# Two-layer attention decoder in float32: the last three heads of layer A projected as q/k of two, q/k of one, values of three; shorter steps in layer A; both transposes ahead of both value products in layer B

## The chip, the cores and the metric

The kernel runs on one core of a Trainium2 chip. The metric is the device time of one execution in microseconds. In the profile PE is TensorE (matrix products), DVE is VectorE, ACT is ScalarE, POOL is GpSimd and SP is the engine that issues all loads of weights.

## The reference

A residual stream of 256 tokens and 1024 columns passes through two layers in float32. Layer A is causal differential attention with 8 heads of 2 x 64 columns, layer B dilated attention in 8 head pairs with three groups of keys; each is followed by an MLP with squared ReLU. Cut to what matters:

```python
# layer A, 8 heads
q, k, v = jnp.split(rms_norm(x, a_norm) @ w_qkv, 3, axis=-1)
q = apply_rope(rms_norm(q, q_gain)); k = apply_rope(rms_norm(k, k_gain))
p = softmax(mask(q @ k.T) * D ** -0.5)          # two maps per head
a = p[:, :, 0] - lam * p[:, :, 1]
o = rms_norm(a @ v, sub_gain) * (1 - lam_init)
x = x + o @ w_o
x = x + square(relu(rms_norm(x, m_norm) @ w_up)) @ w_down
# layer B, three dilation groups; k and v projected from x
o_g, lse_g = softmax attention of group g
o = sum over g of softmax_g(lse)[g] * o_g
x = x + o @ w_o                                   # and the MLP again
```

## The kernel before

Every product of float32 matrices is made of three products of rounded halves: high by high, high by low, low by high (L300 to L302). So each weight tile is split after its load, the high half by ACT (L86) and the low half by VectorE (L87); the same is done with activations (`split`, L346).

Work is driven by the projection. `gemm` (L305) makes one projection in parts; after each part `tick` (L217) is called. A tick splits up to two halves of weights ahead (`W.pump`) and advances each attention generator that is due by one step. A generator `yield`s the number of ticks until its next step, so WAIT_A and WAIT_B say how much projection lies between the steps of a head. The order of TensorE is the order of the code; the orders of the other engines are made by the framework's scheduler, which also may place a `high_priority` piece earlier.

In layer A a head has 48 products of 384 columns (q and k of two maps, 256 columns, and values, 128) with four ticks, one after each 12 products. `rows_A` (`qk_rows`, L317) turns the q/k columns into normed, rotated rows: squares on ACT, a product `T` with the rope table and a reduction on VectorE (L324, L328), then on POOL an add (L335), a power `f` (L339) and a scaling `qn` (L341); there are two such row sets per head, one for each block of 128 tokens. `values_A` splits the values. `attn_A` (L525) has five steps: transposes of q and k on TensorE (L364) and their split `th`, `tl`; scores (L357), mask, exponentials and the combination `smA` (L550); transposes of the softmax weights (L555) and their split `pA`; value products (L566, L567), their sum `orow`, and its norm on POOL (`ms` L578, `ors` L580) and ACT (L582); transposes of the output (L586). Heads 0 to 5 run like this. The last two heads, 6 and 7, have q/k of both in one projection of 512 columns (`Aqk`), then the values of both in one of 256 (`Av`). For a width other than 384 `gemm_half` has one more tick between the two token blocks, so that a step is 6 products of 512 columns or 12 of 256. Then the output projection (`OutProj`, L409 to L411) runs in bodies of 12 products of 512 columns with two ticks each; heads 6 and 7 come last, in `group`.

Layer B goes through 8 head pairs, each with q, k and values of 48 products of 384 columns. `attn_B` (L598): q/k transposes, two steps of scores, then for each of the two heads of the pair transposes of the weights (L629), their split `p`, and the value products (L643), sums on ACT, VectorE and POOL (L646 to L648), and at the end the split `oTh`, `oTl`, which the output projection reads.

PSUM is a pool of eight buffers that all tiles of TensorE's results share; the last values `v` of three heads have three buffers in SBUF.

```python
        yield WAIT_A[0] + 3 * (hd == KT - 1)
...
            yield WAIT_B[4 + hh]
```

Of the kernel before, what the change touches and what calls it, by code (L numbers as in the profile page):

```python
# [16 lines left out]
P = 128  # L17
# [3 lines left out]
KT = DM // P  # L21
HD = 64
# [14 lines left out]

WAIT_A = (3, 2, 4, 3, 4)  # L40
WAIT_B = (4, 2, 2, 5, 3, 3)

SUB = ((2, 0, 4), (3, 1, 5))

# [62 lines left out]
def trunk(ctx, tc, a):  # L107
# [17 lines left out]
    def plan(key, src, n):  # L125
        at[key] = len(chunks)
        chunks.append((src, n))
# [5 lines left out]
            if j > 0:  # L133
                plan(("dn", layer, j - 1), a["wdn"][layer, j - 1], 2 * DM)

    for hd in range(KT - 2):
        for i in range(2):
            plan(("A", hd, i), a["wA"][hd, i], 4 * 384)
    for i in range(2):
        plan(("Aqk", i), a["wAqk"][i], 4 * 512)  # L140
    plan(("Av", 0), a["wAv"], 8 * 256)
    for i in range(4):
        plan(("oA", i), a["woA"][i], 2 * DM)
    plan_mlp(0)
# [72 lines left out]
    def tick():  # L217
        W.pump()
        for ent in list(active):
            if ent[1] > 0:  # L220
                ent[1] -= 1
                continue
            try:
                ent[1] = next(ent[0]) - 1
            except StopIteration:
                active.remove(ent)

    def start(gen):
        ent = [gen, 0]
        active.append(ent)  # L230
        return ent
# [57 lines left out]
    def gemm_half(pss, h, key, j, i, n, nk=2):  # L289

        wh, wl = W.get(at[(*key, j)], i)
        for t in range(NT):
            if t and n != 384:
                tick()
            tok = slice(t * P, (t + 1) * P)
            ps = pss[t][:, :n]
            for k in range(nk):
                kt = nk * (2 * j + i) + k
                c = slice(k * n, (k + 1) * n)
                nc.tensor.matmul(ps, h[:, kt, 0, tok], wh[:, c], start=kt == 0, stop=False)  # L300
                nc.tensor.matmul(ps, h[:, kt, 0, tok], wl[:, c], start=False, stop=False)  # L301
                nc.tensor.matmul(ps, h[:, kt, 1, tok], wh[:, c], start=False, stop=kt == KT - 1)  # L302
        W.release(at[(*key, j)], i)
# [219 lines left out]


    def attn_A(hd, qr, kr, vt, oh, ol):  # L525
        yield WAIT_A[0] + 3 * (hd == KT - 1)
        T = qk_T(qr, kr, (0, P))
        yield WAIT_A[1]
        nm = small.tile([P, 4], F32, name="nm", tag="nm")
        den = small.tile([P, 2, 2], F32, name="den", tag="den")  # L530
        sm = wk.tile([P, 2, 3 * P], F32, name="smA", tag="sm")
        scs = [wps(), wps()]
        scores2([sc[:, 0:S] for sc in scs], T, block(1), KALL)
        scores2([sc[:, S:S + P] for sc in scs], T, block(0), slice(S, S + P))
        for c in range(2):
            sc = scs[c]
            masked(sm[:, c, 0:S], sc[:, 0:S], mask[:, 8:10, :].rearrange("p b k -> p (b k)"),
                   nm[:, 2 + c:3 + c])
            masked(sm[:, c, S:S + P], sc[:, S:S + P], mask[:, 9, :], nm[:, c:c + 1])
        for c in range(2):  # L540
            for q, cols in ((1, slice(0, S)), (0, slice(S, S + P))):
                nc.scalar.activation(sm[:, c, cols], sm[:, c, cols], AF.Exp, bias=nm[:, 2 * q + c:2 * q + c + 1],
                                     scale=-1.0, accum_out=den[:, q, c:c + 1])

        cf = small.tile([P, 2, 2], F32, name="cf", tag="cf")
        nc.vector.reciprocal(cf[:, :, 0], den[:, :, 1])
        nc.vector.scalar_tensor_tensor(cf[:, :, 0], cf[:, :, 0], nlam, den[:, :, 0], op0=ALU.mult, op1=ALU.mult)
        nc.scalar.activation(cf[:, :, 1], den[:, :, 0], AF.Square, scale=EPS ** 0.5)
        for q, cols in ((1, slice(0, S)), (0, slice(S, S + P))):
            nc.vector.scalar_tensor_tensor(sm[:, 0, cols], sm[:, 1, cols], cf[:, q, 0:1], sm[:, 0, cols],  # L550
                                           op0=ALU.mult, op1=ALU.add)
        yield WAIT_A[2]
        pp = wps()
        for i in range(3):
            nc.tensor.transpose(pp[:, block(i)], sm[:, 0, block(i)], ident)  # L555
        p2 = wk.tile([P, 2, 3, P], F32R, name="pA", tag="p2")
        ph, pl = p2[:, 0], p2[:, 1]
        with tc.high_priority(100):
            split(ph, pl, pp[:, :384].rearrange("p (b q) -> p b q", b=3))
        yield WAIT_A[3]  # L560
        po = wps()
        for q in range(2):
            o2 = po[:, q * 2 * P:(q + 1) * 2 * P]
            for j in range(q + 1):
                b = j if q else 2
                nc.tensor.matmul(o2, ph[:, b], vt[:, j], start=j == 0, stop=False)  # L566
                nc.tensor.matmul(o2, pl[:, b], vt[:, j], start=False, stop=j == q)  # L567
        pov = po.rearrange("p (q l d) -> p q l d", q=2, l=2)
        oc = wk.tile([P, 2, P], F32, name="oc", tag="sq")
        nc.scalar.activation(oc, pov[:, :, 1, :], AF.Copy)  # L570
        orow = wk.tile([P, 2, P], F32, name="orow", tag="oT")
        nc.vector.tensor_tensor(orow, pov[:, :, 0, :], oc, op=ALU.add)
        oss = small.tile([P, 2], F32, name="oss", tag="oss")
        for q in range(2):
            nc.scalar.activation(oc[:, q, :], orow[:, q, :], AF.Square, scale=P ** -0.5,
                                 accum_out=oss[:, q:q + 1])
        ms = small.tile([P, 8], F32, name="ms", tag="ms")
        nc.gpsimd.tensor_tensor(ms[:, :2], oss, cf[:, :, 1], op=ALU.add)  # L578
        ors = small.tile([P, 2], F32, name="ors", tag="ors")
        nc.gpsimd.tensor_tensor(ors, ms[:, :2], half[:, :2], op=ALU.pow)  # L580
        for q in range(2):
            nc.scalar.activation(orow[:, q, :], orow[:, q, :], AF.Copy, scale=ors[:, q:q + 1])  # L582
        yield WAIT_A[4]
        pt = wps()
        for q in range(2):
            nc.tensor.transpose(pt[:, block(q)], orow[:, q, :], ident)  # L586

        ptv = pt[:, :S].rearrange("p (m h l) -> p h m l", h=2, l=2)
        for t in range(NT):
            o = oh[:, hd, block(t)].rearrange("p (m l) -> p m l", l=2)  # L590
            nc.scalar.activation(o, ptv[:, t], AF.Copy, scale=sgain)
            nc.vector.scalar_tensor_tensor(ol[:, hd, block(t)].rearrange("p (m l) -> p m l", l=2), ptv[:, t], sgain,
                                           o.bitcast(F32), op0=ALU.mult, op1=ALU.subtract)
# [4 lines left out]
    def attn_B(hp, qr, kr, vts, oh, ol):  # L598
# [4 lines left out]
        for b in range(2):  # L603
# [16 lines left out]
                nc.scalar.activation(sms[hh][:, b, :], sms[hh][:, b, :], AF.Copy, scale=rd[:, hh:hh + 1])  # L620
            yield WAIT_B[2 + b]
        oT = wk.tile([P, S], F32, name="oT", tag="oT")
        for hh in range(2):
            rows = slice(hh * HD, (hh + 1) * HD)
            p2 = wk.tile([P, 2, 4, 2, P], F32R, name="p2", tag="p2")
            for b in range(2):
                pp = wps()
                for i in range(4):
                    nc.tensor.transpose(pp[:, block(i)], sms[hh][:, b, block(i)], ident)  # L629
                with tc.high_priority(100):  # L630
                    split(p2[:, b, :, 0], p2[:, b, :, 1], pp.rearrange("p (i q) -> p i q", i=4))
            yield WAIT_B[4 + hh]

            po = wps()
            pv = po.rearrange("p (l b q) -> p b l q", l=2, b=2)
# [41 lines left out]
    def values_tile():  # L677
        return wk.tile([P, NT, 2, P], F32R, name="v", tag="v", bufs=3)

    for hd in range(KT - 2):  # L680
        vt = values_tile()
        pss = gemm(h, ("A", hd), 384)
        qns = rows_A(pss, 0)
        values_A(pss, 4 * HD, vt)
        tick()
        if hd == 0:
            nc.sync.dma_start(x, a["xp"].rearrange("(t p) d -> p t d", p=P))
            lambda_()
        gens.append(start(attn_A(hd, qns, qns, vt, oh, ol)))

    pss = gemm(h, ("Aqk",), 512)
    vt2 = [values_tile() for _ in range(2)]
    for e in range(2):
        qns = rows_A(pss, e * 4 * HD)
        gens.append(start(attn_A(KT - 2 + e, qns, qns, vt2[e], oh, ol)))
    tick()
    pss = gemm(h, ("Av",), 256, 4)
    for e in range(2):
        values_A(pss, e * P, vt2[e])
    tick()  # L700
    op = OutProj("oA", oh, ol)
    for kt in range(KT - 2):
# [92 lines left out]
def _layout(i):  # L795
# [13 lines left out]
    a["lamv"] = np.stack([np.stack([i["a_lam_q1"][0], i["a_lam_k1"][0]]),  # L809
                          np.stack([i["a_lam_q2"][0], i["a_lam_k2"][0]])])  # L810
    w = np.asarray(i["a_w_qkv"])[0].reshape(2, 4, P, 3, KT, P)
    a["wA"] = w.transpose(4, 0, 2, 1, 3, 5).reshape(KT, 2, P, 4 * 384)[:KT - 2]
    a["wAqk"] = w[:, :, :, :2, KT - 2:].transpose(0, 2, 1, 4, 3, 5).reshape(2, P, 4 * 512)
    a["wAv"] = w[:, :, :, 2, KT - 2:].transpose(2, 0, 1, 3, 4).reshape(P, 8 * 256)

    def kt2(w):
        return np.asarray(w).reshape(4, 2, P, DM).transpose(0, 2, 1, 3).reshape(4, P, 2 * DM)
# [33 lines left out]
```

## Time and profile before

| | us |
|---|---|
| median of 3 runs (807.71 to 808.93) | 808.57 |
| the profiled execution | 808.49 |
| its span, first to last instruction | 806.7 |
| TensorE busy | 774.9 (96%) |
| VectorE busy | 584.0 (72%) |
| ACT busy | 469.5 (58%) |
| POOL busy | 207.8 (26%) |
| mean granted clock of TensorE | 0.989 |

Layer A's attention with its output projection takes the first 150 us, the MLP of layer A follows until some 330 us, layer B's attention until some 625, its MLP to the end. A matrix product is shown with a modelled end, so that a row's duration is longer than the distance to the next row; where rows are compared, the distance between their starts counts. What stands in brackets behind a row is the idle time of the engine before it and what ended it. A wait for several things is put down to the one that came last.

### The profile page before, as it was taken

The page shows a single profiled execution, that of the slowest core. Times are in us where ns is not written, and L with a number is a line of the kernel's source. Part 1 is how long each engine was busy: PE and PEld are TensorE (multiplying, and loading weights), DVE is VectorE, ACT ScalarE, POOL GpSimd, SP SyncE. Part 2 cuts the span into 40 slices and gives each one's busy share as a digit, 9 for nine tenths or more (in the row PEclk, how much of TensorE's full clock was granted, in tenths as well). Part 3 has the DMA queues.
Part 4 walks back from the last instruction along what each step waited for, and adds up shares of the span by engine and source line. Part 5 has one row for each costly group of instructions (what it writes and reads, how often), then busy time and mean ns, then how long its engine had stood idle before and what let it go on. Part 6 is the DMA issues. An engine that isn't in the chain of part 4 may idle for free.

```text
span 806.7 us, 11724 instructions
## 1 busy us (share of the span) xinstructions
PE 774.9 (96%) x4408; PEld 691.2 (86%) x4408; DVE 584.0 (72%) x943; ACT 469.5 (58%) x857; POOL 207.8 (26%) x199
## 2 busy tenths in 40 slices
PE   6998878999999999999999999999998999999998
PEld 6988756788888888899999999999986888888886
DVE  4898776766656665887898898989875766666663
ACT  5667666644454454756676676765875544444441
POOL 2454360400000000064374454648410000000000
PEclk9999899999999999999999999999999999999999
DMA  8644414355545544354443534434532555545531
GB/s 324 224 156 139 149 54 156 109 183 195 203 171 200 188 179 169 122 198 151 157 134 118 181 118 157 165 113 155 197 133 87 201 169 205 190 178 207 175 139 52
DMA packets 22184, 131.12 MB, mean 163 GB/s; under 512 B 2544, under 2 KB 3312, under 8 KB 12528
## 3 DMA queue, kind: packets, MB, share of 16 engines
q1 hardware_dynamic: 22128, 130.38, 45.8%
q8 instruction: 34, 0.56, 0.3%
q14 instruction: 22, 0.18, 0.1%
HBM read 129.32 MB, written 1.05 MB: 162 GB/s over the span
## 4 chain that ended last, share of the span: by engine, by line
PE 83%; DVE 8%; issue 3%; ACT 3%; POOL 2%; DMA 1%; SPq 0%; POOLq 0%; DVEq 0%
PE wps L442 15%; PE acc L300 9%; PE acc L302 9%; PE acc L301 9%; PE wps L444 7%; PE acc L496 7%; PE acc L495 7%; PE acc L494 7%; PE wps L357 3%; DVE wlo L87 2%; PE wps L643 2%; PE acc L409 2%; PE acc L411 1%; PE acc L410 1%; PE wps L629 1%
## 5 line engine op out<-in xcount | busy, mean ns | idle before, releaser
L87 DVE TENSOR_TENSOR wlo<-raw,whi 128x1024 fp32r<-128x1024 f32 (+1 forms) x270 | 306.4, 1138 | 162.5 <-ACT whi L86 162.3
L86 ACT ACTIVATE whi<-raw 128x1024 fp32r<-128x1024 f32 (+1 forms) x270 | 258.3, 963 | 232.7 <-issue 73.0
L442 PE MATMUL wps<-hT,whi 128*128 128x512 f32 x512 | 183.2, 400 | 1.3 <-DVE hT L277 1.3
L444 PE MATMUL wps<-hT,wlo 128*128 128x256 f32 x512 | 143.6, 280 | 0.0
L442 PEld LDWEIGHTS wps<-hT,whi 128*128 128x128 f32 x512 | 96.2, 188 | 26.5 <-DVE hT L277 2.6
L496 PE MATMUL acc<-whi,u 128*128 128x512 f32 x256 | 99.8, 390 | 0.5 <-DVE u L348 0.5
L494 PE MATMUL acc<-whi,u 128*128 128x512 f32 x256 | 100.0, 391 | 0.0
L495 PE MATMUL acc<-wlo,u 128*128 128x512 f32 x256 | 100.0, 391 | 0.0
L444 PEld LDWEIGHTS wps<-hT,wlo 128*128 128x128 f32 x512 | 96.7, 189 | 1.1
L300 PE MATMUL acc<-whi,hT 128*128 128x384 f32 (+2 forms) x256 | 90.4, 353 | 0.0
L302 PE MATMUL acc<-whi,hT 128*128 128x384 f32 (+2 forms) x256 | 87.5, 342 | 0.7 <-DVE hT L277 0.7
L301 PE MATMUL acc<-wlo,hT 128*128 128x384 f32 (+2 forms) x256 | 87.4, 342 | 0.0
L300 PE MATMUL acc<-whi,hK 128*128 128x384 f32 x256 | 87.3, 341 | 0.0
L302 PE MATMUL acc<-whi,hK 128*128 128x384 f32 x256 | 85.8, 335 | 0.0
L301 PE MATMUL acc<-wlo,hK 128*128 128x384 f32 x256 | 85.7, 335 | 0.0
L339 POOL TENSOR_TENSOR f<-ms,half 128x6 f32<-128x6 f32 (+1 forms) x48 | 72.3, 1513 | 16.2 <-DVE ms L330 14.4
L335 POOL TENSOR_TENSOR T<-T 128x384 f32<-128x384 f32 (+1 forms) x48 | 46.0, 959 | 117.0 <-DVE T L324 117.0
L496 PEld LDWEIGHTS acc<-whi,u 128*128 128x128 f32 x256 | 48.1, 188 | 11.5 <-DVE u L348 1.4
L494 PEld LDWEIGHTS acc<-whi,u 128*128 128x128 f32 x256 | 48.1, 188 | 10.5
L495 PEld LDWEIGHTS acc<-wlo,u 128*128 128x128 f32 x256 | 48.1, 188 | 8.8
L300 PEld LDWEIGHTS acc<-whi,hT 128*128 128x128 f32 x256 | 49.4, 193 | 1.9 <-ACT hT L274 0.3
L302 PEld LDWEIGHTS acc<-whi,hT 128*128 128x128 f32 x256 | 49.2, 192 | 1.9 <-DVE hT L277 1.0
(115 smaller groups left out, 1229.0 us busy)
## 6 DMA issues: line engine op xcount, KB each, us to landing
raw<-in_wB SPq DMA_DIRECT2D x48, 768.0 KB, 4.1
raw<-in_wup SPq DMA_DIRECT2D x32, 1024.0 KB, 4.8
raw<-in_wdn SPq DMA_DIRECT2D x32, 1024.0 KB, 4.8
raw<-in_wA SPq DMA_DIRECT2D x11, 768.0 KB, 5.8
raw<-in_woA SPq DMA_DIRECT2D x4, 1024.0 KB, 4.8
raw<-in_woB SPq DMA_DIRECT2D x4, 1024.0 KB, 4.7
raw<-in_wAqk SPq DMA_DIRECT2D x2, 1024.0 KB, 4.8
early<-in_x SPq DMA_DIRECT2D x2, 512.0 KB, 5.4
```

Of the source, the lines that this page charges most:

```text
L86: self.nc.scalar.activation(hi[:, :n], raw, AF.Copy)
L87: self.nc.vector.tensor_tensor(lo[:, :n], raw, hi[:, :n].bitcast(F32), op=ALU.subtract)
L300: nc.tensor.matmul(ps, h[:, kt, 0, tok], wh[:, c], start=kt == 0, stop=False)
L301: nc.tensor.matmul(ps, h[:, kt, 0, tok], wl[:, c], start=False, stop=False)
L302: nc.tensor.matmul(ps, h[:, kt, 1, tok], wh[:, c], start=False, stop=kt == KT - 1)
L335: nc.gpsimd.tensor_tensor(u[:, :n].rearrange("p (h a d) -> p h a d", a=2, d=HD // 2), T[:, 0, :n].rearrange("p (h a d) -> p h a d", a=2, d ...
L339: nc.gpsimd.tensor_tensor(f[:, :nsub], ms[:, :nsub], half[:, :nsub], op=ALU.pow)
L442: nc.tensor.matmul(o, wh[:, c], self.h[:, kt].rearrange("p l s -> p (l s)"), start=kt == 0, stop=False, skip_group_check=True)
L444: nc.tensor.matmul(o[:, 0:S], wl[:, c], self.h[:, kt, 0, :], start=False, stop=kt == KT - 1, skip_group_check=True)
L494: nc.tensor.matmul(ps, uh[:, tok], dh[:, c], start=first, stop=False)
L495: nc.tensor.matmul(ps, uh[:, tok], dl[:, c], start=False, stop=False)
L496: nc.tensor.matmul(ps, ul[:, tok], dh[:, c], start=False, stop=last)
```

## The change

Layer A: heads 0 to 4 are projected as before. The q/k columns of heads 5 and 6 are one projection of 512 columns (`Aqk`), those of head 7 one of 256 (`Aqk1`), and then the values of heads 5 to 7 are one of 384 (`Av`). The extra tick of `gemm_half` moves: it now comes only where a part spans four row blocks (the one of 256 columns), once, after 6 products. A step is thus 12 products of 512 columns in `Aqk`, and 6 or 18 of 256 in `Aqk1`. The steps of a head are 2, 2, 4, 2, 3 ticks, and one or two more ahead of the first for heads 5 to 7.

Layer B: the weights of both heads of a pair are transposed, one tick apart, and two ticks later come the first head's value products, one more tick later the second's. The steps of a pair add up to 17 ticks instead of 19.

```diff
-WAIT_A = (3, 2, 4, 3, 4)
-WAIT_B = (4, 2, 2, 5, 3, 3)
+WAIT_A = (2, 2, 4, 2, 3)
+WAIT_B = (4, 2, 2, 5, 1, 2, 1)
...
-    for hd in range(KT - 2):
+    for hd in range(KT - 3):
         for i in range(2):
             plan(("A", hd, i), a["wA"][hd, i], 4 * 384)
     for i in range(2):
         plan(("Aqk", i), a["wAqk"][i], 4 * 512)
-    plan(("Av", 0), a["wAv"], 8 * 256)
+    plan(("Aqk1", 0), a["wAqk1"], 8 * 256)
+    for i in range(2):
+        plan(("Av", i), a["wAv"][i], 4 * 384)
...
         for t in range(NT):
-            if t and n != 384:
-                tick()
             tok = slice(t * P, (t + 1) * P)
             ps = pss[t][:, :n]
             for k in range(nk):
+                if k == 2 and t == 0:
+                    tick()
                 kt = nk * (2 * j + i) + k
...
     def attn_A(hd, qr, kr, vt, oh, ol):
-        yield WAIT_A[0] + 3 * (hd == KT - 1)
+        yield WAIT_A[0] + (hd >= KT - 3) + (hd == KT - 2)
...
+        p2s = []
         for hh in range(2):
-            rows = slice(hh * HD, (hh + 1) * HD)
             p2 = wk.tile([P, 2, 4, 2, P], F32R, name="p2", tag="p2")
+            p2s.append(p2)
             for b in range(2):
...
             yield WAIT_B[4 + hh]
+        for hh in range(2):
+            if hh:
+                yield WAIT_B[6]
+            rows, p2 = HALVES[hh], p2s[hh]
...
-    for hd in range(KT - 2):
+    for hd in range(KT - 3):
...
-    pss = gemm(h, ("Aqk",), 512)
-    vt2 = [values_tile() for _ in range(2)]
-    for e in range(2):
-        qns = rows_A(pss, e * 4 * HD)
-        gens.append(start(attn_A(KT - 2 + e, qns, qns, vt2[e], oh, ol)))
-    tick()
-    pss = gemm(h, ("Av",), 256, 4)
-    for e in range(2):
-        values_A(pss, e * P, vt2[e])
+    vt3 = [values_tile() for _ in range(3)]
+    for heads, key, n, nk in (((0, 1), ("Aqk",), 512, 2), ((2,), ("Aqk1",), 256, 4)):
+        pss = gemm(h, key, n, nk)
+        for c, e in enumerate(heads):
+            qns = rows_A(pss, c * 4 * HD)
+            gens.append(start(attn_A(KT - 3 + e, qns, qns, vt3[e], oh, ol)))
+        tick()
+    pss = gemm(h, ("Av",), 384)
+    for e in range(3):
+        values_A(pss, e * P, vt3[e])
```

The host's layout of the weights follows (`wA` of five heads, `wAqk`, `wAqk1`, `wAv`).

Three places where the order of an engine moves. The numbers of lines differ by two between the kernels, and by seven or eight in the main part. First VectorE in layer A: head 2's `tl` (L348, after the change L350) and head 3's products `T` with the rope table (L324, L326). Before:

```order
L324 TENSOR_TENSOR T<-acc,tabA 128x2x256
L328 TENSOR_REDUCE ss<-sq 128x4
L550 SCALAR_TENSOR_TENSOR smA<-smA,cf 128x256
L550 SCALAR_TENSOR_TENSOR smA<-smA,cf 128x128
L324 TENSOR_TENSOR T<-acc,tabA 128x2x256
L328 TENSOR_REDUCE ss<-sq 128x4
L87 TENSOR_TENSOR wlo<-raw,whi 128x768
L330 TENSOR_SCALAR ms<-ss,rA 128x4
L348 TENSOR_TENSOR tl<-wps,th 128x512
```

After the change:

```order
L552 SCALAR_TENSOR_TENSOR smA<-smA,cf 128x256
L552 SCALAR_TENSOR_TENSOR smA<-smA,cf 128x128
L87 TENSOR_TENSOR wlo<-raw,whi 128x768
L574 TENSOR_TENSOR orow<-wps,oc 128x256
L350 TENSOR_TENSOR tl<-wps,th 128x512
L326 TENSOR_TENSOR T<-acc,tabA 128x2x256
L330 TENSOR_REDUCE ss<-sq 128x4
```

`tl` stood behind both products of the next head, and now stands ahead of them. Second POOL at the end of layer A, from the first add (`T`) of the heads that share a projection on; `ms` and `ors` are the norm of an earlier head's output. Before (heads 6 and 7):

```order
L335 TENSOR_TENSOR T<-T 128x256
L339 TENSOR_TENSOR f<-ms,half 128x4
L341 TENSOR_TENSOR qn<-T,f 128x256
L335 TENSOR_TENSOR T<-T 128x256
L339 TENSOR_TENSOR f<-ms,half 128x4 x2
L341 TENSOR_TENSOR qn<-T,f 128x256
L578 TENSOR_TENSOR ms<-oss,cf 128x2
L335 TENSOR_TENSOR T<-T 128x256
L580 TENSOR_TENSOR ors<-ms,half 128x2
L341 TENSOR_TENSOR qn<-T,f 128x256
```

After the change (heads 5 and 6):

```order
L337 TENSOR_TENSOR T<-T 128x256 x2
L341 TENSOR_TENSOR f<-ms,half 128x4 x2
L343 TENSOR_TENSOR qn<-T,f 128x256 x2
L341 TENSOR_TENSOR f<-ms,half 128x4
L337 TENSOR_TENSOR T<-T 128x256
L341 TENSOR_TENSOR f<-ms,half 128x4
L337 TENSOR_TENSOR T<-T 128x256
L343 TENSOR_TENSOR qn<-T,f 128x256 x2
L580 TENSOR_TENSOR ms<-oss,cf 128x2
L582 TENSOR_TENSOR ors<-ms,half 128x2
```

The norm of the earlier output stood among the row steps of the last head, and now stands behind all four row sets. Third ACT at the end of layer B's attention: the splits `p` of the last pair's transposes, `ot` behind its value products, and `oTh`, which the output projection waits for. Before:

```order
L347 ACTIVATE p_6605<-wps 128x4x128 x2
L347 ACTIVATE oTh<-oT 128x256
L86 ACTIVATE whi<-raw 128x1024
L646 ACTIVATE ot<-wps 64x512
L347 ACTIVATE p_6659<-wps 128x4x128 x2
L86 ACTIVATE whi<-raw 128x1024 x2
L646 ACTIVATE ot<-wps 64x512
L347 ACTIVATE oTh<-oT 128x256
```

After the change:

```order
L349 ACTIVATE p_6605<-wps 128x4x128 x2
L349 ACTIVATE p_6630<-wps 128x4x128 x2
L86 ACTIVATE whi<-raw 128x1024
L653 ACTIVATE ot<-wps 64x512
L86 ACTIVATE whi<-raw 128x1024
L653 ACTIVATE ot<-wps 64x512
L86 ACTIVATE whi<-raw 128x1024
L349 ACTIVATE oTh<-oT 128x256
```

Both pairs of splits now stand ahead of both `ot`, and one split of weights lies between the last `ot` and `oTh`.

## Rows read from the trace of the kernel before

**Rows 1.** TensorE's waits, whole span: us in total, times, longest us.

```profile
PE wps L357 <- DVE tl L348: 6.2, 5, 2.4
PE wps L586 <- ACT orow L582: 5.4, 2, 3.9
PE acc L409 <- ACT oTh L347: 2.7, 1, 2.7
PE wps L357 <- DVE v L674: 1.6, 2, 1.4
PE wps L364 <- POOL qn L341: 1.2, 1, 1.2
PE wps L555 <- DVE smA L550: 0.9, 2, 0.7
```

**Rows 2.** Busy time by stretch: us, then PE, PEld, DVE, ACT, POOL; PEclk, DMA.

```profile
40.00:83.00 43.00, 36.62 (x239) 34.41 (x237) 38.69 (x95) 30.04 (x84) 21.12 (x25) 1.00 0.45 159
360.00:590.00 230.00, 229.96 (x1551) 222.41 (x1550) 197.35 (x321) 159.31 (x280) 120.75 (x96) 1.00 0.43 151
84.60:89.40 4.80, 4.80 (x15) 3.80 (x14) 2.48 (x11) 2.39 (x11) 2.54 (x4) 0.50 0.66 218
114.00:117.40 3.40, 3.38 (x21) 2.97 (x21) 1.03 (x3) 1.69 (x7) 0.12 (x1) 0.53 0.00 0
141.00:144.20 3.20, 3.20 (x10) 2.45 (x9) 1.37 (x4) 1.09 (x3) 0.00 (x0) 0.52 0.00 0
615.60:618.80 3.20, 3.15 (x8) 2.48 (x8) 1.12 (x2) 0.72 (x2) 0.00 (x0) 0.50 0.00 0
```

**Rows 3.** Timeline of TensorE in layer A: start, us, line; idle before.

```profile
82.93 0.46 PE L357 MATMUL wps<-th,tl 64*128 64x256 f32 x1 [2.39 <-DVE tl L348]
...
114.02 0.77 PE L586 MATMUL wps<-ident,orow 128*128 128x128 f32 x2 [3.90 <-ACT orow L582]
...
123.45 0.39 PE L357 MATMUL wps<-th,tl 64*128 64x256 f32 x2 [1.24 <-DVE tl L348]
...
139.62 0.62 PE L586 MATMUL wps<-ident,orow 128*128 128x128 f32 x2 [1.53 <-ACT orow L582]
```

**Rows 4.** Timeline of TensorE, layer B's output projection.

```profile
612.04 0.40 PE L409 MATMUL acc<-whi,oTh 128*128 128x512 f32 x1
...
612.28 0.39 PE L410 MATMUL acc<-wlo,oTh 128*128 128x512 f32 x1
...
615.64 0.79 PE L409 MATMUL acc<-whi,oTh 128*128 128x512 f32 x1 [2.74 <-ACT oTh L347]
```

**Rows 5.** Groups of instructions by line: row steps of layer A on POOL.

```profile
L339 POOL TENSOR_TENSOR f<-ms,half 128x4 f32<-128x4 f32 x16 | 17.3, 1090 | 6.7 <-DVE ms L330 6.1
...
L341 POOL TENSOR_TENSOR qn<-T,f 128x256 f32<-128x256 f32 x16 | 13.1, 825 | 0.6
...
L335 POOL TENSOR_TENSOR T<-T 128x256 f32<-128x256 f32 x16 | 12.7, 796 | 33.1 <-DVE T L324 33.1
```

**Rows 6.** Timelines of VectorE and of POOL from 106 us on.

```profile
106.34 1.44 DVE L87 TENSOR_TENSOR wlo<-raw,whi 128x1024 fp32r<-128x1024 f32 x1
...
106.65 1.72 POOL L335 TENSOR_TENSOR T<-T 128x256 f32<-128x256 f32 x1
```

**Rows 7.** Timeline of TensorE: one head's steps between projection products.

```profile
91.97 0.38 PE L586 MATMUL wps<-ident,orow 128*128 128x128 f32 x2
...
92.11 0.36 PE L566 MATMUL wps<-v,pA 128*128 128x256 f32 x1
...
92.90 0.39 PE L300 MATMUL acc<-whi,hT 128*128 128x512 f32 x1
...
94.29 0.49 PE L555 MATMUL wps<-ident,smA 128*128 128x128 f32 x3
...
94.71 0.39 PE L357 MATMUL wps<-th,tl 64*128 64x256 f32 x2
...
95.55 0.50 PE L300 MATMUL acc<-whi,hT 128*128 128x512 f32 x1
```

More of the change, by code (lines that the diff above doesn't have):

```diff
@@ L811, in _layout @@
     w = np.asarray(i["a_w_qkv"])[0].reshape(2, 4, P, 3, KT, P)
-    a["wA"] = w.transpose(4, 0, 2, 1, 3, 5).reshape(KT, 2, P, 4 * 384)[:KT - 2]
-    a["wAqk"] = w[:, :, :, :2, KT - 2:].transpose(0, 2, 1, 4, 3, 5).reshape(2, P, 4 * 512)
-    a["wAv"] = w[:, :, :, 2, KT - 2:].transpose(2, 0, 1, 3, 4).reshape(P, 8 * 256)
+    a["wA"] = w.transpose(4, 0, 2, 1, 3, 5).reshape(KT, 2, P, 4 * 384)[:KT - 3]
+    a["wAqk"] = w[:, :, :, :2, KT - 3:KT - 1].transpose(0, 2, 1, 4, 3, 5).reshape(2, P, 4 * 512)
+    a["wAqk1"] = w[:, :, :, :2, KT - 1].transpose(2, 0, 1, 3, 4).reshape(P, 8 * 256)
+    a["wAv"] = w[:, :, :, 2, KT - 3:].transpose(0, 2, 1, 3, 4).reshape(2, P, 4 * 384)
     def kt2(w):
@@ L844 @@
     aps["out"] = nc.dram_tensor("out_x", (S, DM), F32, kind="ExternalOutput").ap()
-    with tile.TileContext(nc, schedule_with_timeline_sim=True) as tc, tc.manual_schedule(engines={mybir.EngineType.PE}):
+    with tile.TileContext(nc, schedule_with_timeline_sim=True) as tc, \
+            tc.manual_schedule(engines={mybir.EngineType.PE}):
         trunk(tc, aps)
```

## Prediction

> **What bounds the kernel now.** I read the waits of TensorE first, then busy time and granted clock by stretch, then the single waits in TensorE's timeline, and last the other engines around them. TensorE is busy for 96% of the span, and in layer B's attention without a gap: 229.96 of 230 us [rows 2]. So a change of order can only win back the waits that are left. They are few: the waits list [rows 1] gives 6.2 us for the low halves of transposed q/k (L348), 5.4 for the scaled output rows (L582), 1.6 for a buffer that layer A's values still hold (L674), 1.2 for q/k rows from POOL and 0.9 for softmax weights, all of them in layer A, and 2.7 for the last head of layer B. To each long wait belongs a second loss: after it the granted clock stands at half, 1.2 GHz, for a while. Four stretches show it [rows 2]: 4.8 us at 0.50, 3.4 at 0.53, 3.2 at 0.52, and 3.2 at 0.50 in layer B. Length times what is missing of the clock makes 2.4, 1.6, 1.5 and 1.6 us.
>
> In the middle of layer A TensorE is not alone: from 40 to 83 us VectorE is busy for 38.69 of 43 us, TensorE for 36.62 [rows 2]. A wait there is partly VectorE's queue, and no order of TensorE's removes that.
>
> The sum is made against the profiled execution: 808.49 us, of which 806.7 are its span; the median of the three runs, 808.57, is 0.08 above it.
>
> **The change, part by part.** The products are the same in number and width, before and after: 288 of 384 columns, 48 of 512 and 48 of 256 in layer A's projection, and the weights are the same bytes in the same count of loads. SP's loads keep their order, so nothing there moves past anything. All that changes is what lies between a step and the step that needs it, and what stands ahead of it in the queues of VectorE, ACT and POOL.
>
> *Heads 0 to 3.* Before, three waits for `tl` and one for `v` fall here: 6.2 - 2.39 - 1.24 = 2.6 [rows 1, 3] and 1.4, together 4.0 us. Head k's q/k transposes now come one step earlier, so that VectorE makes `tl` ahead of the next head's products with the rope table, not behind them (first pair of orders). That takes the reason for the wait away, but VectorE's load stays. Bounds: nothing won (VectorE sets the pace) and 4.0. I take the middle, **-2.0**, because VectorE has 43 - 38.69 = 4.3 us idle in this stretch, as much as these waits, but not where they fall.
>
> *Head 4.* The wait of 2.39 at 82.93 [rows 3] and 0.2 more for `v` come where a step is only 6 products of 512 columns, and then the clock falls for 4.8 us (2.4 lost). Now a step is 12 such products, 12 x 0.24 = 2.9 us [rows 4], and VectorE has `tl` of this head before the first rows of heads 5 and 6. I take all of it, **-5.0**; if the wait itself stays and only the slow clock goes, or the reverse, it is -2.5.
>
> *The end of layer A.* Before: 0.9 + 1.2 + 3.90 + 1.24 + 1.53 = 8.8 us of waits [rows 1, 3], and 1.6 + 1.5 for the clock: 11.9 us. The 3.90 arises on POOL, where the norm of head 4's output (`ms`, `ors`) stood between the row steps of heads 6 and 7 (second pair of orders). After the change I count from the end of the q/k products of heads 5 and 6. POOL then has four row sets in series. One costs 0.80 + 1.09 + 0.83 = 2.7 us [rows 5], so with 0.5 us, which is my assumption, until the first can begin head 5 is ready at 5.9 and head 6 at 11.3. TensorE meanwhile has 30 products of 256 columns (estimate: half of the 0.24 of 512 columns, 3.6 us), the weights' transposes (0.42), scores (0.84), output transposes (0.14) and values (0.79) [rows 7]: it comes to head 5's transposes at 5.8, about when they are ready, and after them and 18 more products, 2.2 us, to head 6's at 8.4. The wait is **2.9 us**: new, and what is late is POOL. Head 7's scores come next: between its q/k transposes and its scores stand 12 products of 384 columns (2.1, an estimate by three quarters of 0.24), 6 of 512 (1.4) and 0.42, so 3.9 us; ahead of its `tl` on VectorE stand the softmax steps of two heads and two weight splits. I take a wait of 2.2, between none and the 3.90 of the longest such wait. Two short ones (`smA` of head 7, `orow` of head 5) at 0.7 each, the longest for softmax weights [rows 1], make 1.4; the outputs of heads 6 and 7 have 18 products or more behind them and should not wait. With one slow stretch of 2.4 this end loses 8.9, against 11.9: **-3.0**. Bounds: 4.3 us lost (POOL's wait and the short ones alone), -7.6; 16.4 us lost (both long new waits doubled, two slow stretches), +4.5.
>
> *Layer B.* Between the value products of the last head pair and the first product that needs its result there are three products of the output projection, from 612.04 on, and then the wait of 2.74 until 615.64 [rows 4]. The steps of a pair now add up to 17 instead of 19, and the last two of them lie behind the value products: 12 more products, 12 x 0.24 = 2.9 us. The whole way from 612.04 to 615.64 was 3.6 us; 15 products cover 3.6. So the wait goes but for some 0.2, and the slow clock behind it (1.6): **-4.1**. Bounds: -4.3, and -2.7 if the clock falls anyhow. In the other pairs the transposes of both heads now follow each other 12 products apart, and the four splits with them; 24 products of 384 columns (4.2 us) remain ahead of the values, and TensorE had no wait here [rows 2], so I cost this at nothing. What hides it is VectorE's slack, 197.35 busy of 230; if that is gone, see the last rival.
>
> Sum: -2.0 - 5.0 - 3.0 - 4.1 = -14.1, and 808.49 - 14.1 = **794.4 us**.
>
> **The rivals.**
> (a) *VectorE sets the pace of layer A.* Its work is the same and must fit into a shorter time; a wait removed then comes back at the next step. For it: 38.69 of 43 us busy from 40 to 83 us [rows 2]. Against it: the 3.90 and the 1.53 have POOL's steps ahead of them, not VectorE's [rows 3]. Heads 0 to 3 then bring nothing, head 4 only 2.5, the end nothing: 808.49 - 2.5 - 4.1 = **801.9 us**.
> (b) *VectorE and POOL hold each other up.* While VectorE split weights from 106.34 on, an add of POOL begun at 106.65 took 1.72 us [rows 6] instead of its mean of 0.80 [rows 5]. The change sets four row sets in a row beside splits; if half of their eight adds and scalings lose 1.72 - 0.80 = 0.9 us each, head 6's transposes come 3.6 us later: 794.4 + 3.6 = **798.0 us**. The Trainium skill (SBUF — State Buffer, section "Who interferes with whom") has a rule that speaks against the change here: a VectorE instruction with two inputs in SBUF and a GpSimd instruction that reads SBUF take turns, the later one waiting for the whole of the other. The pair of rows agrees with it: the add, begun inside the split, is longer by 0.92.
> (c) *Layer B's part does nothing*, since the last result is late by as much as it is moved up: 794.4 + 4.1 = **798.5 us**.
> (d) *All new waits stay small*: -4.0 - 5.0 - 7.6 - 4.3 gives **787.6 us**.
> (e) *Slower: layer B's splits crowd.* The second transposes of each pair come 12 products, 2.1 us, after the first, and ask for two more of the eight PSUM buffers while VectorE still splits the first pair. If TensorE has to wait for that buffer in each of the eight pairs, it decides from 14.1 / 8 = 1.8 us a pair; at 2.3 us it would be 794.4 + 18.4 = **812.8 us**. Against it: 33 us of VectorE's 230 are free, and the values stand 4.2 us further on.
>
> **How the numbers follow.** The forecast has 0.53, (a) 0.20, (b) 0.10, (c) 0.04, (d) 0.10, (e) 0.03. The range 787 to 803 us holds the forecast, (b), (c), most of (d) and most of (a); outside are (e), the upper part of (a) and the lowest of (d), some 0.15. What a measurement here can tell from no change is 0.2%, 1.6 us. Faster by more than that are all but (e) and the upper edge of (a): 0.94; within it 0.03, the upper edge of (a); slower 0.03, which is (e).
>
> **What would show it.** Right: no wait of scores for `tl` between 40 and 90 us and no stretch at half clock there; a wait of about 2.9 us of head 6's q/k transposes for `qn`; no wait at layer B's last output projection and a granted clock of 1.00 there; TensorE still gapless in layer B's pairs. Layer A's output projection would end some 10 us earlier than now, and layer B's part would bring 4 more. Wrong: if the waits for `tl` stay with VectorE above 95% busy it is (a); if POOL's adds grow to 1.2 us and more in the tail, (b); a wait at L629's transposes in layer B is (e).

## The result and the profile after

The changed kernel takes **789.57 us** (median of 4 runs, 788.60 to 790.02), the kernel before in the same comparison 808.43 (807.71 to 808.93): a ratio of 0.9766, 95% interval 0.9749 to 0.9783. The forecast was 794.4 in a range of 787 to 803. The gain is 18.9 us where 14.1 were forecast, nearer to rival (d), all new waits small, than to the sum. The profiled execution took 790.02 us with a span of 788.2; against 808.49 that is 18.5 less, and the parts below are counted against this.

In later runs the kernel before spread over 801.6 to 808.8 us (medians 804.2 to 804.9), the changed one in eight runs over 788.6 to 790.0 only. The gain against those medians is 14 to 15 us (a ratio of 0.9818, interval 0.9797 to 0.9839, in the repetition). That it is close to the 14.1 of the forecast is luck: the forecast was summed against the long execution of 808.49, and there the gain is 18.5.

TensorE's waits in the changed kernel, whole span; total, times, longest in us:

```profile
PE wps L268 <- DMA early<-in_x: 7.2, 2, 5.5
PE wps L366 <- POOL qn L343: 3.8, 3, 2.2
...
PE acc L411 <- ACT oTh L349: 0.8, 1, 0.8
...
PE acc L413 <- DVE oTl L350: 0.6, 1, 0.6
...
PE acc L411 <- DVE pA L350: 0.3, 1, 0.3
PE wps L359 <- DVE tl L350: 0.2, 1, 0.2
PE wps L588 <- ACT v L680: 0.2, 1, 0.2
```

Against [rows 1]: the waits for `tl` fall from 6.2 to 0.2 us, those for `orow` (5.4) and `v` at the scores (1.6) are gone, the one for `oTh` falls from 2.7 to 0.8. One line has grown: q/k rows from POOL, 1.2 before, 3.8 now. The clock and the load by stretch (us, then PE, PEld, DVE, ACT, POOL; PEclk, DMA share, GB/s):

```profile
40.00:83.00 43.00, 43.00 (x283) 39.58 (x282) 40.10 (x106) 32.86 (x96) 24.74 (x29) 1.00 0.46 160
84.00:92.00 8.00, 5.56 (x34) 5.16 (x33) 8.00 (x16) 4.88 (x16) 7.82 (x10) 0.86 0.38 134
89.40:93.00 3.60, 3.60 (x15) 3.60 (x14) 3.60 (x7) 1.18 (x3) 3.50 (x5) 0.56 0.04 16
580.00:610.00 30.00, 28.16 (x145) 22.82 (x144) 21.27 (x33) 19.98 (x36) 2.21 (x3) 1.00 0.33 121
```

From 40 to 83 us TensorE has no gap now (36.62 of 43 before [rows 2]), with VectorE busy for 40.10 where it was 38.69: more work in the same time, and no wait. Of the four slow stretches of [rows 2] one is left, 3.6 us at 0.56, behind the longest wait; layer B's end runs at 1.00. The mean granted clock went from 0.989 to 0.998.

The single waits in TensorE's timeline (start, us; idle before):

```profile
39.03 0.44 PE L366 MATMUL wps<-ident,qn 128*128 128x128 f32 x2 [1.33 <-POOL qn L343]
...
88.54 0.33 PE L366 MATMUL wps<-ident,qn 128*128 128x128 f32 x1 [2.15 <-POOL qn L343]
89.16 0.55 PE L366 MATMUL wps<-ident,qn 128*128 128x128 f32 x3 [0.29 <-POOL qn L343]
...
105.31 0.38 PE L359 MATMUL wps<-th,tl 64*128 64x256 f32 x2 [0.20 <-DVE tl L350]
```

The first belongs to head 1 and was not forecast; the second is the wait that was forecast, at head 6's q/k transposes; the third is head 7's scores. POOL ahead of the second (start, us, operation):

```profile
77.84 0.74 POOL L337 TENSOR_TENSOR T<-T 128x256 f32<-128x256 f32 x1
79.01 0.73 POOL L337 TENSOR_TENSOR T<-T 128x256 f32<-128x256 f32 x1 [0.42 <-DVE T L326]
79.85 2.64 POOL L341 TENSOR_TENSOR f<-ms,half 128x4 f32<-128x4 f32 x2
82.46 1.18 POOL L343 TENSOR_TENSOR qn<-T,f 128x256 f32<-128x256 f32 x2
83.61 1.00 POOL L341 TENSOR_TENSOR f<-ms,half 128x4 f32<-128x4 f32 x1
84.58 1.47 POOL L337 TENSOR_TENSOR T<-T 128x256 f32<-128x256 f32 x1
86.01 1.02 POOL L341 TENSOR_TENSOR f<-ms,half 128x4 f32<-128x4 f32 x1
87.00 0.73 POOL L337 TENSOR_TENSOR T<-T 128x256 f32<-128x256 f32 x1
87.69 1.42 POOL L343 TENSOR_TENSOR qn<-T,f 128x256 f32<-128x256 f32 x2
```

Four row sets in a row, two heads with two token blocks each, from 77.84 to 89.11: 11.3 us with one gap of 0.42. TensorE waits here for POOL, as forecast.

Where the 18.5 us came from, by the start of the same work in both traces. The first products of layer A's MLP and of layer B's, each before and after the change:

```profile
148.20 0.40 PE L442 MATMUL wps<-hT,whi 128*128 128x512 f32 x1
133.45 0.40 PE L444 MATMUL wps<-hT,whi 128*128 128x512 f32 x1
...
623.00 0.40 PE L442 MATMUL wps<-hT,whi 128*128 128x512 f32 x1
604.45 0.39 PE L444 MATMUL wps<-hT,whi 128*128 128x512 f32 x1
```

The MLP of layer A begins 14.75 us earlier, the first product of layer B 14.75 earlier (315.50 against 330.25), the MLP of layer B 18.55 earlier. So layer A's attention brought 14.75 and layer B's 3.8; the rest of the program moved as it was.

### The profile page after: what moved, and what is told of

Read it like the earlier page. It is cut to its first block, busy times and chain, and to the rows that moved or that the text cites. A ratio compares the mean times of both kernels' runs of the same rounds, so it can differ in the third digit from the quotient of the medians.

```text
span 788.2 us, 11720 instructions
## 1 busy us (share of the span) xinstructions
PE 768.8 (98%) x4408; PEld 686.4 (87%) x4408; DVE 578.4 (73%) x943; ACT 469.8 (60%) x857; POOL 201.8 (26%) x199
## 4 chain that ended last, share of the span: by engine, by line
PE 90%; DVE 5%; ACT 2%; POOL 1%; issue 1%; DMA 1%; SPq 0%; DVEq 0%; ACTq 0%
PE wps L444 15%; PE acc L302 11%; PE acc L304 10%; PE acc L303 10%; PE wps L446 8%; PE acc L498 7%; PE acc L497 7%; PE acc L496 7%; PE wps L359 3%; PE wps L650 2%; PE wps L632 2%; PE wps L366 2%; DVE wlo L87 2%; PE acc L413 1%; PE acc L411 1%; PE acc L412 1%
## 5 line engine op out<-in xcount | busy, mean ns | idle before, releaser
L341 POOL TENSOR_TENSOR f<-ms,half 128x6 f32<-128x6 f32 (+1 forms) x48 | 69.7, 1461 | 12.0 <-DVE ms L332 11.0
L337 POOL TENSOR_TENSOR T<-T 128x384 f32<-128x384 f32 (+1 forms) x48 | 47.9, 997 | 83.1 <-DVE T L326 83.0
L498 PEld LDWEIGHTS acc<-whi,u 128*128 128x128 f32 x256 | 48.1, 188 | 11.3 <-DVE u L350 1.2
```

Of the source, the lines that this page charges most:

```text
L337: nc.gpsimd.tensor_tensor(u[:, :n].rearrange("p (h a d) -> p h a d", a=2, d=HD // 2), T[:, 0, :n].rearrange("p (h a d) -> p h a d", a=2, d ...
L341: nc.gpsimd.tensor_tensor(f[:, :nsub], ms[:, :nsub], half[:, :nsub], op=ALU.pow)
L498: nc.tensor.matmul(ps, ul[:, tok], dh[:, c], start=False, stop=last)
```

## The experiments

Each was timed beside the kernel before. Theory 1: the shorter steps take the waits for `tl` away from heads 0 to 3, the new grouping saves head 4 and the end of layer A, the 17 ticks save layer B's end. Its rivals stand with each run.

**The two layers apart.** `a_only` is the change with layer B's `attn_B` and `WAIT_B` as before; `b_only` is the kernel before with those two as changed.

```diff
 # a_only, against the change
-WAIT_B = (4, 2, 2, 5, 1, 2, 1)
+WAIT_B = (4, 2, 2, 5, 3, 3)
 # b_only, against the kernel before
-WAIT_B = (4, 2, 2, 5, 3, 3)
+WAIT_B = (4, 2, 2, 5, 1, 2, 1)
```

> Layer A as changed, layer B as before. If the two parts add up and each gives what the traces show for its stretch (14.75 us up to the first product of layer B, 3.7 behind it), 808.4 - 14.75 = 793.7 us, and the wait of 2.7 us for oTh with its slow clock is back. If layer B's change did nothing (the gain behind layer A comes from elsewhere) it is 789.6.

Measured 793.08 us (792.37 to 793.41): as theory 1 had it, to 0.6 us. The wait of 2.74 for `oTh` is back, and 789.57 against 793.08 makes layer B's part 3.5 us.

> Layer B as changed, layer A as before. If the parts add up, 808.4 - 3.7 = 804.7 us. If layer B's gain depends on when layer A ends it is 808.4; if the splits of both heads crowd, above 810.

Measured 801.62 us (799.72 to 805.09), a ratio of 0.9963 (0.9940 to 0.9987) to 804.93 of the kernel before: 3.3 us. The parts add up, and the splits do not crowd.

This run told something else. Its layer A is the old one, with the same order of instructions on every engine, yet its profiled execution reaches the MLP of layer A at 143.50 us, 4.7 earlier than the profile of the kernel before. Up to 70 us it is only 0.64 ahead. Stretches and one wait of it:

```profile
66.00:76.00 10.00, 7.69 (x42) 7.15 (x41) 7.89 (x23) 6.01 (x23) 6.89 (x7) 0.83 0.30 107
84.60:89.40 4.80, 4.80 (x28) 4.07 (x27) 2.11 (x13) 2.78 (x11) 1.91 (x4) 1.00 0.62 224
```

```profile
82.30 0.38 PE L357 MATMUL wps<-th,tl 64*128 64x256 f32 x1 [0.81 <-DVE tl L348]
```

The half clock lies some eleven microseconds earlier here (0.83 on average from 66 to 76 us; 1.00 from 84.6 to 89.4, where the profile of before had 0.50). Head 4's scores begin, with `tl` ready, at 82.30 against 82.93, still 0.64 ahead. But TensorE, slowed, has come to them 1.6 us later by the same measure, and the wait is 0.81 us, not the 2.39 of [rows 3]. Here the half clock fell ahead of a wait, which hid its loss; in the profile of before it fell behind the wait, and its loss came on top. So the same instructions give different times by where the clock falls among their waits. That the kernel before spreads over 7 us and the changed one, with few waits left, over 1.4, agrees with this. So do the twelve executions of `b_only`: the five with a mean clock of 0.994 took 799.7 to 800.5 us, the three with 0.989 took 804.9 to 805.1. But the four with 0.991 lie anywhere from 800.8 to 804.7, so that the mean clock alone does not give the time; that the place of the fall gives the rest is argued from this one pair of profiles and was not tried.

> The changed kernel once more, beside more runs of the kernel before. The kernel before spread over 801.6 to 808.6 us in the last call; if that spread belongs to its own late tl at head 4 (2.39 us and the slow clock in the one profile, 0.81 and none in another), the changed kernel, which has no such wait, stays within 1.5 us of 789.6. If it is the chip's, the changed kernel spreads by 5 us or more as well.

Measured 789.77 us (789.02 to 789.87), beside 802.69 to 808.72 of the kernel before on the same chip: the spread belongs to the old kernel, not to the chip.

**Steps and grouping of layer A apart.** Both runs keep layer B as changed, so `b_only` is the corner with neither.

```diff
 # a_old_steps, against the change
-WAIT_A = (2, 2, 4, 2, 3)
+WAIT_A = (3, 2, 4, 3, 4)
 # a_old_group, against b_only
-WAIT_A = (3, 2, 4, 3, 4)
+WAIT_A = (2, 2, 4, 2, 3)
```

> The change, but layer A's steps 3 2 4 3 4 as before; the new grouping stays. Theory 1 (shorter steps take away the waits for tl of heads 0 to 3, the grouping does head 4 and the end): the three waits for tl and the one for v come back, 4.0, and the wait of 1.6 for qn at head 1 goes: 789.6 + 2.4 = 792.0 us. Theory 2 (the steps do nearly all of layer A's gain): 789.6 + 12 = 801.6 or more, with the wait for orow of 3.9 back.

> The change, but layer A's last heads grouped as before (q/k of two, values of two, the tick between the token blocks); the steps 2 2 4 2 3 stay. Theory 1: head 4's loss (5.0) and most of the end's (11.9 against 4.9 now) come back: 789.6 + 8 to 12 = 797.6 to 801.6 us. Theory 2 (the steps do nearly all): 789.6 + 2.4 = 792 us.

| us, median | old grouping | new grouping |
|---|---|---|
| steps 3 2 4 3 4 | 801.62 | 794.57 |
| steps 2 2 4 2 3 | 796.12 | 789.57 |

Neither theory: the grouping brings 7.1 us with the old steps and 6.6 with the new, the steps 5.5 and 5.0. They add up, and each is about half (the corner of 801.62 spreads by 5 us, so the numbers beside it are good to some 2). The waits say why both are needed. First `a_old_steps`, then `a_old_group`:

```profile
PE wps L359 <- DVE tl L350: 2.3, 3, 1.0
PE acc L411 <- DVE tl L350: 2.1, 1, 2.1
PE wps L359 <- DVE v L681: 1.3, 1, 1.3
```

```profile
PE wps L364 <- POOL qn L341: 7.8, 5, 3.2
PE wps L586 <- ACT orow L582: 1.1, 2, 0.8
```

With late transposes TensorE waits for what VectorE makes behind them (`tl`); with early ones it waits for what POOL makes ahead of them (`qn`), five times, up to 3.2 us. In the main the shorter steps move a wait, from behind the transposes to ahead of them. With the old grouping the waits of layer A over 0.15 us, those for the input apart, add up to 13.0 us in the profile of `b_only` and still to 11.0 in that of `a_old_group`; the clock stands at half for some 10 us of layer A in the first and for 3.4 in the second. With the new grouping the waits for `qn` are 3.8 us instead of 7.8.

**The longer steps alone.** The extra tick back to its old place:

```diff
         for t in range(NT):
+            if t and n != 384:
+                tick()
             tok = slice(t * P, (t + 1) * P)
...
-                if k == 2 and t == 0:
-                    tick()
```

> The change, but the extra tick stands between the two token blocks again, for all widths but 384: steps of 6 products of 512 columns while heads 5 and 6 are projected, of 12 of 256 for head 7. If the longer steps are what saved head 4, its wait for tl (2.4 us in the profile of the kernel before, 0.8 in another execution) and a slow clock come back: 791 to 794.4 us. If tl ahead of the next rows on VectorE saved it, nothing of this comes back: 789.6.

Measured 797.59 us (794.24 to 799.18): 8.0 lost, more than the text ahead of the run had under either reading. And it is not `tl` that comes back:

```profile
PE wps L366 <- POOL qn L343: 8.2, 4, 2.9
PE wps L588 <- ACT orow L584: 0.9, 2, 0.7
```

```profile
92.00:104.00 12.00, 9.10 (x44) 8.08 (x44) 5.57 (x9) 4.16 (x7) 8.58 (x12) 0.57 0.06 25
```

Four waits for `qn`, 8.2 us where the change has 3.8, which is 4.4 more. TensorE is busy for 9.10 of the 12 us at a clock of 0.57, which costs 9.1 x 0.43 = 3.9 us against 3.6 x 0.44 = 1.6, another 2.3. With the waits for `orow` (0.9, none in the change) that makes 7.6, and the two profiled executions are 7.5 apart. Two of the six executions had the mean clock of the changed kernel, 0.998, and took 794.24 and 794.93: some 5 us are lost without any more slow clock. So the 12 products to a step buy time for POOL's row sets. I had put their worth down to VectorE's `tl`; with the shorter steps, what they hide is POOL. Longer pieces with the old steps were not tried.

**What is left at the end of layer A.** Three tries on the two waits for `qn`.

```diff
 # h6_later
-        yield WAIT_A[0] + (hd >= KT - 3) + (hd == KT - 2)
+        yield WAIT_A[0] + (hd >= KT - 3) + 2 * (hd == KT - 2)
 # h1_later
-        yield WAIT_A[0] + (hd >= KT - 3) + (hd == KT - 2)
+        yield WAIT_A[0] + (hd >= KT - 3) + (hd == KT - 2) + (hd == 1)
```

> The change, but head 6's q/k transposes (and all its later steps) one tick later, behind 12 products of 384 columns, 2.1 us. If the wait of 2.15 us for qn from POOL is what is left of the end of layer A, the wait and the half clock behind it (0.86 of full speed over 8 us) go: 789.6 - 3.8 = 785.8 us. Rival: head 6 then ends later and its scores meet those of head 7 on VectorE; the loss comes back in the output projection, 789.6 us.

Measured 789.04 us (788.71 to 789.36): 0.7 less than the 789.77 beside it, with runs that overlap, so mostly the rival. The wait at head 6 and the slow clock are gone (1.00 from 83 to 108 us), but other waits come behind them, for head 7's `qn` (1.68 us; the other wait of that line is head 1's), for a buffer that the last values still hold, and for the low halves of an output:

```profile
83.00:108.00 25.00, 22.48 (x156) 19.89 (x156) 23.41 (x67) 20.41 (x64) 15.20 (x17) 1.00 0.36 127
...
PE wps L366 <- POOL qn L343: 3.0, 2, 1.7
PE wps L557 <- DVE v L681: 1.4, 1, 1.4
PE acc L413 <- DVE oTl L594: 0.8, 1, 0.8
```

VectorE is busy for 23.41 of these 25 us (22.52 in the change). I take it that this leaves an order little to win, but no run here makes VectorE's work less.

> The change, but head 1's q/k transposes (and all its later steps) one tick later. If the wait of 1.33 us for qn at 37 us is only that the step comes too early, it goes: 789.6 - 1.6 = 788.0 us. Rival: then tl is behind the next head's products on VectorE again, a wait of 0.96 for tl comes back at head 1's scores: 789.0 us.

Measured 793.12 us (792.94 to 794.06): 3.4 lost, against both. The wait at 37 us goes, and two longer ones come, 2.16 us at 60.7 and 3.03 at 91.4, both for `qn`. At the first, POOL itself had waited for VectorE (POOL's row, then VectorE's):

```profile
58.88 1.01 POOL L341 TENSOR_TENSOR f<-ms,half 128x4 f32<-128x4 f32 x1 [1.30 <-DVE ms L332]
```

```profile
57.08 1.58 DVE L87 TENSOR_TENSOR wlo<-raw,whi 128x1024 fp32r<-128x1024 f32 x1
58.59 0.22 DVE L332 TENSOR_SCALAR ms<-ss,rA 128x4 f32<-128x4 f32 x1
```

A small `ms` of four columns stands behind a weight split of 1.58 us. Moving the steps of one head by 12 products changed what stands ahead of the steps of later heads; one cannot take a wait out by its own row alone.

The third try moves work off POOL: the scaling `qn` of heads 5 and 6 goes to ACT, with 16 ticks in layer B (next paragraph), so that it compares with that run's 788.74.

```diff
-        nc.gpsimd.tensor_tensor(
...
+        if on_act:
+            for e in range(nsub):
+                hc = slice(e * HD, (e + 1) * HD)
+                nc.scalar.activation(qn[:, hc], u[:, hc], AF.Copy, scale=f[:, e:e + 1])
+        else:
+            nc.gpsimd.tensor_tensor(
...
-            qns = rows_A(pss, c * 4 * HD)
+            qns = rows_A(pss, c * 4 * HD, len(heads) == 2)
```

> 16 ticks in layer B (788.7 us in its own run) and the scaling qn of heads 5 and 6 on ACT, four instructions of 64 columns each, in place of one of 256 on POOL; all else is the change. If POOL's series of four row sets is what the wait of 2.14 us at head 6's transposes and its slow clock come from, POOL has some 2 us less ahead of it: 788.7 - 3.8 = 784.9 us. If VectorE sets the pace there (busy for 8.00 of 8 us from 84 to 92 us), the wait passes to another place: 788 to 789.

Measured 788.83 us (787.15 to 789.29): nothing gained. The wait passed on, to ACT's `qn` and to `tl`. The profiled execution is one of the two short ones, 787.37 us, and even it has 3.8 us of these two waits, where the change has 3.2 at this end:

```profile
PE wps L371 <- ACT qn L346: 2.2, 3, 1.1
PE wps L364 <- DVE tl L355: 1.6, 1, 1.6
```

POOL alone is therefore not the bound of this end: when POOL is relieved, a row of ACT's and one of VectorE's come late instead.

**Layer B: ticks or order.** `b_order` keeps the old order of transposes and value products, with 17 ticks; `b_16` keeps the new order with 16.

```diff
 # b_order: attn_B as before the change, and
-WAIT_B = (4, 2, 2, 5, 1, 2, 1)
+WAIT_B = (4, 2, 2, 5, 3, 1)
 # b_16
-WAIT_B = (4, 2, 2, 5, 1, 2, 1)
+WAIT_B = (4, 2, 2, 5, 1, 1, 1)
```

> The change, but layer B's second head is transposed behind the first head's value products as before, with 17 ticks in all (4 2 2 5 3 1): value products of the second head one tick, 12 products of 384 or 6 of 512 columns, behind its transposes. If the early transposes are needed to have 17 ticks, the splits p are late in the tail (1.4 us of cover where two splits on ACT and two on VectorE take over 2): a wait of about 1 us at the last value products and its delay to oTh, 790.5 us; with 2.1 us of cover in the pairs before no wait there. If the count of ticks alone matters, 789.6.

Measured 789.44 us (789.03 to 790.18), the same as the change. Two waits for the splits `p` appear (0.91 us at 543.7 us in a pair, 0.38 at 593.6 in the tail; about 1 us was expected, in the tail only), and those for `oTh` and `oTl` (0.82 and 0.56 in the change) are gone instead. The transposes ahead of the value products bring nothing by themselves; the two ticks less do.

> The change, but a pair of layer B takes 16 ticks: the first value products one tick behind the second transposes. If the ticks behind the value products are what layer B's part brings, the last result gets 6 more products of 512 columns (1.4 us) of cover, the waits of 0.82 and 0.56 us go: 789.6 - 1.4 = 788.2 us. Rival: the splits p are late instead, a wait at the value products (L650) in eight pairs, over 791.

Measured 788.74 us (787.14 to 788.80), 1.0 below the 789.77 of the change beside it, with no wait for `oTh` and none at the value products. In its trace the MLP of layer B starts 1.35 us earlier than in the changed kernel's, where 1.4 were expected.

**Both together.** `h6_later` and `b_16` in one kernel.

> Head 6 one tick later and 16 ticks in layer B, together. The two act on places 490 us apart; if they add up it is 789.8 - 0.7 - 1.0 = 788.0 us (788.0 of 804.2 to 804.4 before: a ratio of 0.980), with no slow clock between 84 and 108 us and no wait for oTh. If head 6's gain was only the place of the clock's fall, it is 788.7 as with 16 ticks alone.

Measured **787.42 us** (786.50 to 787.70), a ratio of 0.9789 (0.9773 to 0.9805) to 804.27: 2.2 us below the change, whose eight runs lie above all five of these. The sum of 788.0 holds within 0.6 us, which is less than these times can tell. But the clock did fall here, behind the same wait of 1.68 us that had left it at 1.00 in `h6_later`:

```profile
97.40:101.00 3.60, 3.56 (x14) 3.56 (x15) 3.60 (x14) 2.51 (x9) 0.00 (x0) 0.56 0.13 18
```

Even so, this profiled execution is the shortest of the five (786.50), and two longer ones (787.26, 787.42) had a mean clock of 1.00. Part of the loss was hidden: a wait for `pA` behind it is 0.34 us here and 0.84 in `h6_later`.

## Why the prediction was right, and where it was off

*Heads 0 to 3* (forecast -2.0). Measured -2.7: the waits of 4.0 us for `tl` and `v` are gone, one of 1.33 for `qn` at head 1 is new. VectorE's load, for which I took half, was no obstacle, at 40.10 of 43 us. That an earlier transposition has a price of its own on POOL's side was missing from the working. In these heads it is that one wait; `a_old_group` shows it for the later heads, where without the new grouping four more waits for `qn` make 6.5 of its 7.8 us.

*Head 4* (-5.0). No wait and a clock of 1.00 there, so by the prediction's own terms -5.0 against the profile that the sum is made with. Its term for the clock was too small, though: the row of [rows 2] begins 1.5 us after the clock fell and ends before it rose, and the whole stretch of the kernel before is

```profile
83.10:89.90 6.80, 6.61 (x23) 5.17 (x24) 4.14 (x16) 3.51 (x15) 4.04 (x6) 0.50 0.47 157
```

or 3.4 us by the prediction's rule, not 2.4. In the profiled execution of `b_only` this place had 1.1 us of waits and no slow clock behind it, so against such an execution it is worth less. The cause that I named (12 products, for `tl`) was wrong in its second half: `old_tick` shows that with pieces of 6 products what is late is `qn`.

*The end of layer A* (-3.0): **this is the step that was off.** "This end loses 8.9, against 11.9": it loses 4.8, waits of 2.15 + 0.29 + 0.20 + 0.32 + 0.20 = 3.2 and 3.6 x 0.44 = 1.6 for the clock, so it is -7.1. POOL's wait was right in its mechanism and nearly in its size. Counted from the end of the q/k products of heads 5 and 6 (77.49), head 6's rows were ready after 11.6 us (11.3 in the forecast) and TensorE came for them after 8.9 (8.4), which made waits of 2.44 (2.9). What was wrong is "I take a wait of 2.2, between none and the 3.90" for head 7's `tl`: it was 0.20. Between its transposes (until 101.07) and the end of its `tl` (105.26) VectorE has 1.48 us of softmax steps of the two other heads (`smA`), one weight split of 1.22, and `oTl`, `orow` and `tl` itself with 0.34, 0.41 and 0.68: 4.1 us of these 4.2. I had given TensorE 3.9 until it asks, and it asked after 4.0. I had named what stands ahead of `tl`, but not added it up, and set a middle value in its place. The short waits, 1.4 in the forecast, were 0.5, and the slow stretch cost 1.6 where 2.4 were set. Of the 4.4 us between forecast and profiled execution 4.1 lie here.

The three terms of layer A make 2.7 + 5.0 + 7.1 = 14.8, and the starts of the MLP say 14.75. That this agrees to 0.1 us is partly luck, since the clock behind head 4 was read 1.0 too low. TensorE's busy time up to the MLP, before and after the change, separates the two:

```profile
0.00:148.20 148.20, 125.65 (x720) 112.71 (x721) 109.97 (x262) 95.38 (x261) 56.02 (x74) 0.95 0.46 164
0.00:133.45 133.45, 121.48 (x720) 109.31 (x721) 108.10 (x262) 95.18 (x261) 58.02 (x74) 0.99 0.51 182
```

For the same 720 instructions it is idle for 10.6 us less (22.55 against 11.97) and busy for 4.2 less. With the whole stretch of 6.8 us the prediction's rule gives 3.4 + 1.6 + 1.5 - 1.6 = 4.9 for the clock, somewhat more than those 4.2.

*Layer B* (-4.1). The waits of 0.82 and 0.56 us stayed, where I left 0.2; the slow clock went. By the waits it is 4.3 - 1.4 = 2.9, by the starts 3.8, by the runs without it 3.3 to 3.5; where the 0.9 between the first two lies was not followed. The cover of 15 products was right, the way behind the values was longer than the 3.6 us of before. ACT, VectorE and POOL behind the last value products (start, us, operation):

```profile
593.76 0.60 ACT L653 ACTIVATE ot<-wps 64x512 f32<-64x512 f32 x1
593.77 1.22 DVE L87 TENSOR_TENSOR wlo<-raw,whi 128x1024 fp32r<-128x1024 f32 x1 [1.16 <-ACT whi L86]
...
595.03 0.69 DVE L654 TENSOR_TENSOR ot<-wps,ot 64x512 f32<-64x512 f32 x1
...
595.79 0.74 POOL L655 TENSOR_TENSOR oT<-ot 64x256 f32<-64x256 f32 x1 [2.37 <-DVE ot L654]
...
596.40 1.06 ACT L86 ACTIVATE whi<-raw 128x1024 fp32r<-128x1024 f32 x1 [2.04 <-issue]
...
597.36 0.40 ACT L349 ACTIVATE oTh<-oT 128x256 fp32r<-128x256 f32 x1
```

`oT` is done at 596.53, but ACT has begun a weight split at 596.40, and `oTh` starts at 597.36: 0.8 us, which is the wait. The row of ACT's order that showed this split between the last `ot` and `oTh` stands in the section on the change; I had read it and not priced it.

*The rivals.* (a) VectorE as the pace: not with this change; whether the tries that go further end there (23.41 of 25 us busy in `h6_later`) was not shown. (b) VectorE and POOL hold each other up: the pattern is there. Ahead of head 6's transposes one add of four was long, 1.47 us beside 0.74, and the two `f` at 79.85 took 2.64 where one takes 1.0: 1.4 us in all, and not the 3.6 of the rival. The means of [rows 5] already hold such pairs, so that the four row sets, counted at 10.8, came out at 11.3. The long add began at 84.58, inside a weight split that VectorE had begun at 84.51 and that took 0.94. The rule of the Trainium skill (SBUF — State Buffer, "Who interferes with whom") agrees with that row. (c) and (e) are out by `b_only`. (d), all new waits small, is nearly what happened in layer A, but for POOL's wait.

## What to carry to other kernels

A step's due time has two ends: early, it waits for its inputs' maker, late, the next step waits for its result's maker; read both engines' queues before a step is moved. Where a step comes after a fixed amount of projection, longer pieces give the helper engines more time between steps (in `old_tick` the shorter pieces cost 8.0 us). And a new wait is the difference of two sums, what stands ahead of the result (4.2 us here) and what covers it (4.0); add both up, and don't take a middle between the shortest and the longest wait of the trace.

## What the runs showed that I had not expected

The prediction had a half clock behind each long wait; a wait does not always cost the clock. In the profile of the kernel before, waits of 1.40 us at 70.8 and of 1.24 at 123.5 have no slow stretch behind them, one of 1.53 at 139.6 has. The same wait at the same place can do either: 1.68 us ahead of head 7's transposes left it at 1.00 in `h6_later` and brought 3.6 us at 0.56 in `h6_b16`, and the old layer A has its first half clock from 83.1 us on in one execution, between 66 and 76 in another. The length of the one profiled execution of the kernel before, 808.5 us, stands at the upper end of what it takes (801.6 to 808.9); its waits are therefore one sample, and a forecast from it is one of that execution. What decides where the clock falls was not tried.
